# The two row blocks of the largest expert, cut into small units and spread between the other experts

## The chip, the core and the metric

The kernel runs on one core of one Trainium2 chip. The metric is the device time in microseconds of one execution, as the median of several runs; smaller is better. The core's engines are PE (TensorE, matrix products), DVE (VectorE), ACT (ScalarE), POOL (GpSimd) and SP, whose queue issues the loads of weights; 16 DMA engines move the data. The engines run their own instruction lists in order and wait for one another by semaphores.

## What is computed

The reference runs two transformer blocks on 256 tokens of width 1024, in float32. The change touches the last part only, a mixture of eight experts in which each token goes to two:

```
def moe_swiglu(x, router_w, router_b, w1, w3, w2):
    logits = (x @ router_w) + router_b
    top_vals, top_idx = lax.top_k(logits, TOP_K)          # TOP_K = 2, N_EXPERTS = 8
    top_w = jax.nn.softmax(top_vals, axis=-1)
    gate = jnp.sum(jax.nn.one_hot(top_idx, N_EXPERTS) * top_w[..., None], axis=-2)
    out = jnp.zeros_like(x)
    for e in range(N_EXPERTS):
        out = out + gate[..., e:e + 1] * swiglu(x, w1[e], w3[e], w2[e])
    return out                                            # swiglu: (silu(x w1) * (x w3)) w2
```

`w1` and `w3` of an expert are 1024 x 1408, `w2` is 1408 x 1024: 3 x 1024 x 1408 x 4 bytes = 17.3 MB an expert.

## The kernel before

**Weights.** The class `Weights` streams all weights in the order of a plan that a dry run writes down. `load` (L195) sends a load on SP's queue into the raw ring, as soon as `room_for` finds its slot free. The raw ring is made of arenas: `raw` (8192 columns of 128 partitions in f32), and in the experts' phase also `rawx` (6144), `cpack` (2048) and `rawt` (2048). `convert` splits a piece into a high and a low part: ACT writes `wh` (L232), DVE subtracts and writes `wl` (L233), into one ring of 6144 columns for each part. A piece of `w1` or `w3` here is one row of 128 x 1408, one of `w2` is 128 x 1024. A slot of the raw ring is free again when DVE has read it, one of the converted ring when PE has used it.

**Products.** Tokens are gathered into row blocks. A full block holds 128 tokens and takes three passes of PE for each piece (x high by w high, x high by w low, x low by w high). A half block holds up to 64 tokens, with high and low part side by side, and takes two passes. In the listings L421 to L423 (helper `mm3`) are the passes of full blocks, L1575 and L1576 (`mm_block`) those of half blocks. `turned` transposes the hidden values of a block between `w3` and `w2` (L1590 for half blocks, L1603 for full ones) and splits them again on ACT and DVE.

**Order.** Expert 0 is known before routing and goes first. The others stand in places 0 to 6 by load: place 0 is the largest and has two blocks, a full one (index 0) and a half one (index `NE`); places 1 and 2 have full blocks, places 3 to 6 half blocks. `moe` runs expert 0 and then the places 1, 4, 5, 0, 6, 2, 3 one after the other (list `groups`). `whole` is a generator: the first four rows of `w1` of the next expert run between `w3` and `w2` of the one before, and the work of `turned` is spread over them, one step behind each row (`todo`). For place 0 its loads are groups of 768 or 640 columns, and both blocks use each converted piece at once. Place 3, the last, runs through `expert`, with loads of four rows of 512 columns, and the final sum and norm stand around it.

`fetch` gets a block's rows: POOL makes a one-hot matrix `Pm` (L1489, from `kept` for full blocks and from `half` for half ones), PE multiplies it with the row numbers (`gp`, L1540), DVE copies the result (L1550, L1551), and POOL gathers the rows by an indirect DMA (L1556); after ten further steps PE transposes them (L1564). `route_places` is a chain of small operations on POOL and DVE that wait for each other; the sorting of the places and of the rows of the results (L1441 to L1482) is part of it.

Of the kernel before, what the change touches and what calls it, by code (L numbers as in the profile page):

```python
# [28 lines left out]
P = 128  # L29
# [5 lines left out]
NE = 8  # L35
# [251 lines left out]
class Build:  # L287
# [1243 lines left out]
    def fetch(self, j, out, half=False, back=False):  # L1531
# [28 lines left out]
        xh, xl = self.xslot(), None if half else self.xslot()  # L1560
# [48 lines left out]
    def whole(self, W, blks, w1, w3, w2, places, hT0=None):  # L1609

        nc = self.nc
        nb = len(blks)
        c0 = FFE % 512 if hT0 else 0
        kt = 2 if nb == 2 or hT0 else 1
        groups = [[(c, min(512, FFE - c)) for c in range(c0, FFE, 512)]] if nb == 1 else [
            [(0, 384), (384, 384)], [(768, 384), (1152, 256)]]
        passes = sum(2 if blk[3] else 3 for blk in blks)  # L1620

        def rows(w, ps, cols, k0, k1):
            a = cols[0][0]
            n = sum(m for _, m in cols)
            for kk in range(k0, k1, kt):
                for k, (_, wh, wl) in enumerate(W.want(w, kk * P, kt, a, n), kk):
                    for (x, *_), pb in zip(blks, ps):
                        for p, (c, m) in zip(pb, cols):
                            self.mm_block(p, [v if v is None else v[:, k] for v in x], wh[:, 0, c - a:c - a + m],
                                          wl[:, 0, c - a:c - a + m], k == 0, k == KD - 1)  # L1630
                    W.done()
                    self.tick(0)
                    self.step()
                    if todo:
                        todo.popleft()()

        banks = lambda name, cols: [[self.bank([m], name) for _, m in cols] for _ in blks]
        hT = [[] for _ in blks]
        todo = self.pending

        def evict(ps, h):
            for (_, _, _, half), pb, hb in zip(blks, ps, h):
                for p, r in zip(pb, hb):
                    nc.scalar.activation(r[0], p, AF.Copy if half else AF.Silu)

        def turns(ps, h, cols):

            for (_, _, _, half), pb, hb in zip(blks, ps, h):
                for p, r, (_, m) in zip(pb, hb, cols):
                    if half:  # L1650
                        r.append(self.b2([m], "su"))
                        nc.scalar.activation(r[1], p, AF.Copy)
                    else:
                        nc.vector.tensor_mul(r[0], p, r[0])
            new = deque(self.turned(blks[i][3], r, m, hT[i]) for i, hb in enumerate(h) for r, (_, m) in zip(hb, cols))
            run = []
            while new or run:
                yield
                run = [v for v in run if next(v, "end") != "end"]
                if new:  # L1660
                    run.append(new.popleft())
                    next(run[-1])

        for g, cols in enumerate(groups):
            ps = banks("g", cols)
            k0 = 0
            if g == 0 and not hT0:
                k0 = 4
                todo = yield
                rows(w1, ps, cols, 0, k0)  # L1670
                yield
                todo = self.pending
            rows(w1, ps, cols, k0, KD)
            h = [[[self.b2([m], "sg")] for _, m in cols] for _ in blks]
            if hT0:
                th = hT0()
                hT[0] = [tuple(v[:, k] for v in th) for k in range(c0 // P)]
            while todo:
                todo.popleft()()
# [447 lines left out]
```

## Time and profile before

| what | value |
|---|---|
| time, median of 3 runs | 1344.3 us (1343.62 to 1344.4) |
| time of the profiled execution | 1344.31 us |
| its span, first to last instruction | 1342.5 us |
| PE, DVE, ACT busy in the span | 96%, 71%, 57% |
| mean granted PE clock | 0.994 |
| weights of the experts | 8 x 17.3 MB, from about 890 us on |

The profiled execution is as long as the median run, so its span can stand for the runs, with 1.8 us around it. A busy PE is not PE at its peak: the ends of matrix products are modelled and overlap, so the price of one is read from the distance of two starts. The experts' phase is the last third of the span, from 889.9 us (the first product with expert weights) on.

### The profile page before, as it was taken

What the parts mean: (1) busy time and instruction counts of PE and PEld (TensorE: products, weight loads), DVE (VectorE), ACT (ScalarE), POOL (GpSimd) and SP (SyncE); (2) the same over time, 40 slices, a digit from 0 to 9 for tenths busy, and PEclk for the clock granted to TensorE, in tenths of its full rate; (3) what the DMA queues carried; (4) which work ended last, traced back from release to release, by engine and by line L of the source; (5) the groups of instructions that cost most, each with busy time, mean ns of one, the idle gap of its engine ahead of it and who ended that gap; (6) DMA issues with size and microseconds to landing.
All of it is one profiled execution on the core that took longest, in us unless ns stands there. A gap on an engine that the chain in (4) does not pass through costs nothing. (4 is left out here: it accounts for less than half of the span.)

```text
span 1342.5 us, 20715 instructions
## 1 busy us (share of the span) xinstructions
PE 1293.2 (96%) x7987; PEld 1137.2 (85%) x7987; DVE 956.5 (71%) x1252; ACT 763.0 (57%) x1057; POOL 171.6 (13%) x226
## 2 busy tenths in 40 slices
PE   9999999999999999999999999998999999989994
PEld 6977899997998998999989989987786789868772
DVE  6796565556784878465566866786998986659987
ACT  5674554443664655354434656445688885668882
POOL 3401200001000201000001002027502111001011
PEclk9999999999999999999999999999999999999997
DMA  7635867552562466575545623558999999769993
GB/s 275 204 126 173 307 218 238 189 188 79 182 227 94 158 202 220 174 239 173 187 140 156 219 98 107 192 186 338 331 397 364 373 390 348 259 225 388 391 373 95
DMA packets 128596, 309.59 MB, mean 231 GB/s; under 512 B 7345, under 2 KB 22737, under 8 KB 128490
## 3 DMA queue, kind: packets, MB, share of 16 engines
q1 hardware_dynamic: 121274, 287.65, 61.1%
q0 software_dynamic: 5424, 17.40, 4.4%
q10 hardware_dynamic: 1792, 3.15, 0.6%
q8 instruction: 64, 1.05, 0.3%
q14 instruction: 42, 0.34, 0.1%
HBM read 294.24 MB, written 10.78 MB: 227 GB/s over the span
## 5 line engine op out<-in xcount | busy, mean ns | idle before, releaser
L233 DVE TENSOR_TENSOR wl<-raw,wh 128x1024 fp32r<-128x1024 f32 (+4 forms) x338 | 395.1, 1194 | 157.4 <-ACT wh L232 151.9
L232 ACT ACTIVATE wh<-raw 128x1024 fp32r<-128x1024 f32 (+4 forms) x338 | 339.9, 1029 | 199.1 <-PE tr L495 99.8
L494 PE MATMUL tr<-xTh,wh 128*128 128x256 f32 x816 | 232.5, 285 | 0.0
L496 PE MATMUL tr<-xTh,wl 128*128 128x256 f32 x816 | 230.7, 283 | 0.0
L495 PE MATMUL tr<-xTl,wh 128*128 128x256 f32 x816 | 230.7, 283 | 0.0
L494 PEld LDWEIGHTS tr<-xTh,wh 128*128 128x128 f32 x816 | 156.3, 192 | 1.2
L495 PEld LDWEIGHTS tr<-xTl,wh 128*128 128x128 f32 x816 | 156.3, 192 | 0.5
L496 PEld LDWEIGHTS tr<-xTh,wl 128*128 128x128 f32 x816 | 156.3, 192 | 0.0
L233 DVE TENSOR_TENSOR wl<-rawx,wh 128x1024 fp32r<-128x1024 f32 (+4 forms) x85 | 106.9, 1291 | 16.7 <-ACT wh L232 16.7
L233 DVE TENSOR_TENSOR wx<-raw,wx 128x1024 fp32r<-128x1024 f32 (+1 forms) x56 | 65.6, 1185 | 49.2 <-ACT wx L232 49.2
L232 ACT ACTIVATE wh<-rawx 128x1024 fp32r<-128x1024 f32 (+4 forms) x85 | 91.7, 1110 | 15.1 <-PE u L1575 5.4
L232 ACT ACTIVATE wx<-raw 128x1024 fp32r<-128x1024 f32 (+1 forms) x56 | 56.4, 1030 | 49.2 <-PE tr L495 25.5
L495 PE MATMUL tr<-xTl,wx 128*128 128x256 f32 x240 | 67.5, 281 | 0.0
L494 PE MATMUL tr<-xTh,wx 128*128 128x256 f32 x240 | 67.4, 281 | 0.0
L496 PE MATMUL tr<-xTh,wx 128*128 128x256 f32 x240 | 67.4, 281 | 0.0
L529 POOL TENSOR_SCALAR rs<-lnmv 128x1 f32<-128x1 f32 x10 | 7.8, 782 | 455.4 <-DVE lnmv L576 455.4
L421 PE MATMUL nat<-wh,xTh 128*128 128x512 f32 (+1 forms) x152 | 60.5, 398 | 0.0
L422 PE MATMUL nat<-wl,xTh 128*128 128x512 f32 (+1 forms) x152 | 58.8, 387 | 0.7 <-DVE wl L233 0.4
L423 PE MATMUL nat<-wh,xTl 128*128 128x512 f32 (+1 forms) x152 | 58.7, 386 | 0.1
L1576 PE MATMUL u<-wl,xgh 128*128 128x384 f32 (+1 forms) x104 | 39.5, 384 | 6.3 <-DVE wl L233 6.2
L494 PEld LDWEIGHTS tr<-xTh,wx 128*128 128x128 f32 x240 | 45.2, 189 | 0.1
L495 PEld LDWEIGHTS tr<-xTl,wx 128*128 128x128 f32 x240 | 45.2, 188 | 0.1
(510 smaller groups left out, 3043.0 us busy)
## 6 DMA issues: line engine op xcount, KB each, us to landing
raw<-in_w_in SPq DMA_DIRECT2D x43, 1024.0 KB, 6.7
raw<-in_moe_w SPq DMA_DIRECT2D x44, 704.0 KB, 6.0
raw<-in_ffn_w SPq DMA_DIRECT2D x30, 1024.0 KB, 5.0
rawx<-in_moe_w SPq DMA_DIRECT2D x26, 1024.0 KB, 8.9
raw<-in_moe_w SPq DMA_DIRECT2D x17, 1024.0 KB, 10.1
rawx<-in_moe_w SPq DMA_DIRECT2D x23, 704.0 KB, 9.4
raw<-in_moe_w SPq DMA_DIRECT2D x14, 768.0 KB, 14.4
raw<-in_w_gate SPq DMA_DIRECT2D x10, 1024.0 KB, 5.2
```

The lines of the kernel that those rows point to most:

```text
L232: nc.scalar.activation(hi[:, :kn, :n], src, AF.Copy)
L233: nc.vector.tensor_sub(lo[:, :kn, :n], src, hi[:, :kn, :n])
L421: mm(out, xh, wh, start=start, stop=False)
L422: mm(out, xh, wl, start=False, stop=False)
L423: mm(out, xl, wh, start=False, stop=stop)
L494: mm(o, a, xh[:, kb + k], start=first and j % 2 == 0, stop=False, **kw)
L495: mm(o, a, xl[:, kb + k], start=False, stop=False, **kw)
L496: mm(o, b, xh[:, kb + k], start=False, stop=(kb + k == kt - 1), **kw)
L529: nc.gpsimd.tensor_scalar(out, ms, eps, None, op0=OP.add)
L1576: self.nc.tensor.matmul(out, x[0], wl, start=False, stop=stop)
```

## The change

`whole` is no longer a generator and has one block only. The largest expert (place 0) leaves the list; its two blocks run in a generator of its own, `beside_experts`, in units: two rows of `w1` or `w3` by 512 (or 384) columns, or two rows of `w2` by 512 columns, for both blocks. `fill` adds credit behind each row of another expert (0.17 for a full block, 0.34 for a half one), at the end of `w1` and `w3` (1) and behind each step of `turned` (0.7), and runs one step of the generator for each whole credit, as soon as both blocks are fetched. The order of the others is 4, 1, 5, 2, 6, 3. The first four rows of the next expert no longer run between `w3` and `w2`. The arena `rawx` is gone; the space goes to two more slots for gathered rows (`xs`) and to 22 instead of 14 tiles of 512 columns. Of the loads of expert weights there are 197 instead of 156, since `w2` comes in single rows and place 0 in units.

```
-    def whole(self, W, blks, w1, w3, w2, places, hT0=None):
...
-        kt = 2 if nb == 2 or hT0 else 1
-        groups = [[(c, min(512, FFE - c)) for c in range(c0, FFE, 512)]] if nb == 1 else [
-            [(0, 384), (384, 384)], [(768, 384), (1152, 256)]]
...
-            if g == 0 and not hT0:
-                k0 = 4
-                todo = yield
-                rows(w1, ps, cols, 0, k0)
-                yield
-                todo = self.pending
...
+    def whole(self, W, blk, w1, w3, w2, r0, fill, hT0=None):
+        x, _, gate, half = blk
         c0 = FFE % 512 if hT0 else 0
+        cols = [(c, min(512, FFE - c)) for c in range(c0, FFE, 512)]
+        rate = 0.34 if half else 0.17
+
+        def behind():
+            W.done()
+            self.tick(0)
+            self.step()
+            if self.pending:
+                self.pending.popleft()()
+            fill(rate)
+
+        def rows(w, ps):
+            for k in range(KD):
+                (_, wh, wl), = W.want(w, k * P, 1, c0, FFE - c0)
+                for p, (c, m) in zip(ps, cols):
+                    self.mm_block(p, [v if v is None else v[:, k] for v in x], wh[:, 0, c - c0:c - c0 + m],
+                                  wl[:, 0, c - c0:c - c0 + m], k == 0, k == KD - 1)
+                behind()
+
+        ps = [self.bank([m], "g") for _, m in cols]
+        rows(w1, ps)
+        fill(1)
...
+        ps = [self.bank([m], "u") for _, m in cols]
+        rows(w3, ps)
+        fill(1)
+        for _ in self.turns(blk, ps, h, [m for _, m in cols], hT):
+            fill(0.7)
+        acc = [self.bank([512], "eacc") for _ in range(2)]
+        for k in range(FFE // P):
+            (_, wh, wl), = W.want(w2, k * P, 1, 0, D)
...
+            behind()
...
+    def turns(self, blk, ps, h, ms, hT):
+        for p, r, m in zip(ps, h, ms):
+            self.evict2(blk[3], p, r, m)
+        for r, m in zip(h, ms):
+            yield
+            yield from self.turned(blk[3], r, m, hT)
...
+    def beside_experts(self, W, blks, w1, w3, w2, places):
+        cols = [(c, min(512, FFE - c)) for c in range(0, FFE, 512)]
         hT = [[] for _ in blks]
+        def up(w, name, c, m):
+            ps = [self.bank([m], name) for _ in blks]
+            for k in range(0, KD, 2):
+                (_, wh, wl), = W.want(w, k * P, 2, c, m)
+                for (x, *_), p in zip(blks, ps):
+                    for j in range(2):
+                        self.mm_block(p, [v if v is None else v[:, k + j] for v in x], wh[:, j], wl[:, j],
+                                      k + j == 0, k + j == KD - 1)
                 W.done()
                 self.tick(0)
+                yield
+            return ps
+        for c, m in cols:
+            ps = yield from up(w1, "g", c, m)
...
+            ps = yield from up(w3, "u", c, m)
+            for blk, p, r, t in zip(blks, ps, h, hT):
+                yield from self.turns(blk, [p], [r], [m], t)
+                yield
+        for hf in range(2):
+            acc = [self.bank([512], "eacc") for _ in blks]
+            for k in range(0, FFE // P, 2):
+                kn = min(2, FFE // P - k)
+                (_, wh, wl), = W.want(w2, k * P, kn, hf * 512, 512)
...
     def moe(self, x, xT, T):
-        self.phase("moe", 0, 14, 7)
-        self.W.arenas += [self.tmp.tile([P, 6144], F32, name="rawx", tag="rawx", bufs=1), self.cpack[:, :2048]]
+        self.phase("moe", 0, 22, 7)
+        self.W.arenas.append(self.cpack[:, :2048])
-        groups = [[1], [4], [5], [0, NE], [6], [2], [3]]
+        order = [4, 1, 5, 2, 6, 3]
...
+        tb = self.spawn(late([0, NE], mine, lambda: next(big)))
+        tg = self.spawn(late(order[:1], gots[0], self.xslot, 4))
+        side, credit = [], [0.0]
+
+        def fill(n):
+            if not side and mine and tb not in self.threads:
+                side.append(self.beside_experts(self.W, mine, *[(n, 0, "p0") for n in names], [YROW[0], P]))
+            credit[0] = min(credit[0] + n, 2.0)
+            while side and side[0] and credit[0] >= 1:
+                credit[0] -= 1
+                if next(side[0], "end") == "end":
+                    side[0] = None
```

The first place is on POOL, in the chain of routing behind expert 0's first products (`kept` makes the one-hot matrix of a full block, `half` that of a half one; `ybase` and `yv` belong to the rows of the results).

```order
 L1436 TENSOR_SCALAR pg<-pg 128x2
 L1489 TENSOR_SCALAR Pm<-kept,pg 128x128 x2
+L1489 TENSOR_SCALAR Pm<-half,pg 128x128 x2
 L1441 TENSOR_SCALAR ybase<-kept 128x8
 L1442 MEMSET ybase 128x1
```

The half block of place 0 is now fetched together with the full one, so a second pair of one-hot operations stands ahead of the rest of the chain. A few rows on, POOL also has a second gather and the pair of place 4:

```order
 L1475 COPY route<-route 128x8
+L1489 TENSOR_SCALAR Pm<-half,pg 128x128 x2
 L1478 TENSOR_SCALAR route<-kept,route 128x8
 L1479 TENSOR_TENSOR ptmp<-route 128x40
```

This pair stood behind the whole chain before and now stands within it.

The second place is on PE, in place 0's products with `w2` of the kernel before (10592 and 10593 are the halves of the full block, 10594 and 10595 those of the half one).

```order
L421 MATMUL eacc_10592<-wh_65,hTh_10325 128x512
L422 MATMUL eacc_10592<-wl_69,hTh_10325 128x512
L423 MATMUL eacc_10592<-wh_65,hTl_10326 128x512
L421 MATMUL eacc_10593<-wh_65,hTh_10325 128x512
L422 MATMUL eacc_10593<-wl_69,hTh_10325 128x512
L423 MATMUL eacc_10593<-wh_65,hTl_10326 128x512
L1575 MATMUL eacc_10594<-wh_65,hT_10389 128x512
L1576 MATMUL eacc_10594<-wl_69,hT_10389 128x512
L1575 MATMUL eacc_10595<-wh_65,hT_10389 128x512
L1576 MATMUL eacc_10595<-wl_69,hT_10389 128x512
```

These ten are one row of `w2`, and eleven such rows stand behind one another. In the changed kernel a unit of place 0 (8940 is its full block, 8941 the half one; seven of its ten products stand here) stands between rows of `w1` of place 4 (9069 to 9071):

```order
L421 MATMUL g_8940<-wh_65,xgl_8335 128x512
L422 MATMUL g_8940<-wl_69,xgl_8335 128x512
L423 MATMUL g_8940<-wh_65,xs_8336 128x512
L1575 MATMUL g_8941<-wh_65,xs_8337 128x512
L1576 MATMUL g_8941<-wl_69,xs_8337 128x512
L1575 MATMUL g_8941<-wh_65,xs_8337 128x512
L1576 MATMUL g_8941<-wl_69,xs_8337 128x512
L1575 MATMUL g_9069<-wh_65,xgl_8335 128x512
L1576 MATMUL g_9069<-wl_69,xgl_8335 128x512
L1575 MATMUL g_9070<-wh_65,xgl_8335 128x512
L1576 MATMUL g_9070<-wl_69,xgl_8335 128x512
L1575 MATMUL g_9071<-wh_65,xgl_8335 128x384
```

About every third row of a half block, and every sixth of a full one, such a unit follows. Its first units stand in expert 0's `w2`, its last in `w3` of place 2.

The third place is on PE too, at the turn from `w3` to `w2` of place 5 before (9908 is the transposed part of its hidden values; 9865 to 9868 are products of place 0's first rows).

```order
L1590 MATMUL tp_9908<-half_8328,sg_9787 128x64 x4
L1590 MATMUL tp_9908<-half_8328,su_9887 128x64 x4
L421 MATMUL g_9865<-wh_65,xgl_8333 128x384
L422 MATMUL g_9865<-wl_69,xgl_8333 128x384
L423 MATMUL g_9865<-wh_65,xgl_8333 128x384
L421 MATMUL g_9866<-wh_65,xgl_8333 128x384
L422 MATMUL g_9866<-wl_69,xgl_8333 128x384
L423 MATMUL g_9866<-wh_65,xgl_8333 128x384
```

At the turn of place 4 in the changed kernel (9346, 9372 and 9393 are its own transposes, 9331 and 9360 those of place 0's two blocks, 9400 the next unit's product):

```order
L1603 MATMUL tp_9331<-ident_88,sg_9148 128x128 x4
L1590 MATMUL tp_9346<-half_8330,sg_9216 128x64 x4
L1590 MATMUL tp_9346<-half_8330,su_9336 128x64 x4
L1590 MATMUL tp_9360<-half_8330,sg_9150 128x64 x4
L1590 MATMUL tp_9360<-half_8330,su_9355 128x64 x4
L1590 MATMUL tp_9372<-half_8330,sg_9218 128x64 x4
L1590 MATMUL tp_9372<-half_8330,su_9338 128x64 x4
L1590 MATMUL tp_9393<-half_8330,sg_9220 128x64 x3
L1590 MATMUL tp_9393<-half_8330,su_9340 128x64 x3
L421 MATMUL g_9400<-wh_65,xgl_8335 128x512
```

Place 0 turns at the same point, so the transposes stand behind one another there without a row of products between them.

## Rows read from the trace of the kernel before

**Rows 1.** Page, section 2: 40 slices of the span, DMA in tenths and in GB/s.

```profile
DMA  7635867552562466575545623558999999769993
GB/s 275 204 126 173 307 218 238 189 188 79 182 227 94 158 202 220 174 239 173 187 140 156 219 98 107 192 186 338 331 397 364 373 390 348 259 225 388 391 373 95
```

**Rows 2.** Windows of the experts' phase: stretch, busy time of each engine, clock, DMA.

```profile
core 0: us, PE busy (x) PEld busy (x) DVE busy (x) ACT busy (x) POOL busy (x), PEclk, DMA share, GB/s
...
900.00:960.00 60.00, 54.78 (x295) 47.26 (x294) 45.76 (x80) 37.59 (x46) 37.12 (x72) 1.00 0.88 322
960.00:1130.00 170.00, 164.42 (x833) 136.98 (x832) 145.24 (x143) 133.45 (x157) 31.65 (x18) 1.00 1.01 380
1130.00:1210.00 80.00, 73.73 (x403) 63.19 (x402) 50.50 (x54) 49.37 (x64) 6.14 (x5) 1.00 0.73 251
1210.00:1310.00 100.00, 97.23 (x481) 79.11 (x480) 89.86 (x88) 82.94 (x99) 12.13 (x9) 1.00 1.04 385
1310.00:1320.00 10.00, 8.50 (x38) 5.98 (x38) 8.98 (x11) 7.38 (x11) 1.55 (x1) 1.00 0.60 165
```

**Rows 3.** Timeline of PE, first products behind each expert's last `w2` row (start, duration).

```profile
945.24 0.48 PE L421 MATMUL g<-wh,xgl 128*128 128x512 f32 x1
...
955.06 0.40 PE L421 MATMUL eacc<-wh,hTh 128*128 128x512 f32 x1
...
971.52 0.50 PE L421 MATMUL g<-wh,xgl 128*128 128x512 f32 x1
...
1019.17 0.50 PE L1575 MATMUL g<-wh,xgh 128*128 128x512 f32 x1
...
1063.21 0.50 PE L1575 MATMUL g<-wh,xgh 128*128 128x512 f32 x1
...
1106.52 0.44 PE L421 MATMUL g<-wh,xgl 128*128 128x384 f32 x1
...
1191.25 0.47 PE L1575 MATMUL g<-wh,xgh 128*128 128x512 f32 x1
```

**Rows 4.** Timeline of PE: seven products in succession, and transposes of a half block.

```profile
950.87 0.39 PE L423 MATMUL g<-wh,xgl 128*128 128x512 f32 x1
...
951.78 0.33 PE L421 MATMUL g<-wh,xgl 128*128 128x384 f32 x1
...
952.30 0.50 PE L1540 MATMUL gp<-pg,Pm 128*128 128x2 f32 x4
...
1086.35 1.00 PE L1590 MATMUL tp<-half,sg 128*128 128x64 f32 x8
1087.18 1.06 PE L1590 MATMUL tp<-half,su 128*128 128x64 f32 x8
1088.05 0.42 PE L421 MATMUL g<-wh,xgl 128*128 128x384 f32 x1
```

**Rows 5.** Groups by line and form, 880 us on: DVE's share of a conversion.

```profile
L233 DVE TENSOR_TENSOR wl<-raw,wh 128x1408 fp32r<-128x1408 f32 x44 | 70.5, 1627 | 21.4 <-ACT wh L232 19.0 <-DMA cpack<-in_moe_w 1.5 <-DMA yd<-y 0.8
L233 DVE TENSOR_TENSOR wl<-rawx,wh 128x1024 fp32r<-128x1024 f32 x53 | 62.8, 1221 | 7.5 <-ACT wh L232 7.5
```

**Rows 6.** Waits of SP's queue from 880 us on: total us, times, longest.

```profile
SPq L195 <- DVE wl L233: 220.0, 110, 22.2
```

**Rows 7.** Timelines of PE, DVE and POOL in the chain of routing.

```profile
924.42 0.38 PE L1540 MATMUL gp<-pg,Pm 128*128 128x2 f32 x2 [1.32 <-POOL Pm L1489]
...
925.89 0.17 DVE L1451 MAX8 yhas<-yv 128x8 f32<-128x8 f32 x1 [1.91 <-POOL yv L1450]
...
921.32 3.05 POOL L1489 TENSOR_SCALAR Pm<-kept,pg 128x128 f32<-128x128 f32 x2
...
931.67 1.89 POOL L1556 DMA_INDIRECT xrows<-xd,islot  x1 [0.82 <-DVE gslot L1551]
...
945.87 2.57 POOL L1489 TENSOR_SCALAR Pm<-half,pg 128x128 f32<-128x128 f32 x2
...
956.72 9.46 POOL L1489 TENSOR_SCALAR Pm<-half,pg 128x128 f32<-128x128 f32 x2
```

More of the change, by code (lines that the diff above doesn't have):

```diff
@@ L1529, in gather, with fetch @@
         nc.scalar.activation(PT, tp.rearrange("p a b -> p (a b)"), AF.Copy)
-    def fetch(self, j, out, half=False, back=False):
+    def fetch(self, j, out, slot, half=False, back=False):
         nc = self.nc
@@ L1559, in fetch @@
             yield
-        xh, xl = self.xslot(), None if half else self.xslot()
+        xh, xl = slot(), None if half else slot()
         for k0 in range(0, KD, 4):
@@ L1718, in whole @@
-        self.pending.extend(lambda i=i, hf=hf: back(i, hf) for i in range(nb) for hf in range(2))
-        yield
+                yield
+            return ps
+        for c, m in cols:
+            ps = yield from up(w1, "g", c, m)
+            h = [[] for _ in blks]
+            for (_, _, _, half), p, r in zip(blks, ps, h):
+                self.evict(half, p, r, m)
+            ps = yield from up(w3, "u", c, m)
+            for blk, p, r, t in zip(blks, ps, h, hT):
+                yield from self.turns(blk, [p], [r], [m], t)
+                yield
@@ new lines, in beside_experts @@
+        for hf in range(2):
+            acc = [self.bank([512], "eacc") for _ in blks]
+            for k in range(0, FFE // P, 2):
+                kn = min(2, FFE // P - k)
+                (_, wh, wl), = W.want(w2, k * P, kn, hf * 512, 512)
+                for p, t in zip(acc, hT):
+                    for j in range(kn):
+                        self.mm_block(p, t[k + j], wh[:, j], wl[:, j], k + j == 0, k + j == FFE // P - 1)
+                W.done()
+                self.tick(0)
+                yield
+            for (_, _, g, half), p, r0 in zip(blks, acc, places):
+                self.back(half, g, p, r0, hf)
@@ L1940, in add, with late @@
             nc.vector.tensor_add(x2[t][:, sl], x2[t][:, sl], comb[t][hf])
-        def late(js, got):
+        def late(js, got, slot, delay=0):
             while not self.placed:
                 yield
-            gens = [self.fetch(j, got, half=3 <= j <= NE, back=j in groups[-1]) for j in js]
+            for _ in range(delay):
+                yield
+            gens = [self.fetch(j, got, slot, half=3 <= j <= NE, back=j == order[-1]) for j in js]
             while gens:
@@ L1966, in moe @@
                 break
-            tg = self.spawn(late(groups[i + 1], fetched[i + 1]))
-            new = self.whole(self.W, got, *ws, [YROW[js[0]], P])
-            next(new)
-            new.send(todo)
-            for _ in run:
-                pass
-            run = new
+            tg = self.spawn(late(order[i + 1:i + 2], gots[i + 1], self.xslot))
+            self.whole(self.W, gots[i][0], *ws, YROW[j], fill)
+        got = gots[-1]
+        last = self.expert(self.W, got, *ws)
+        next(last)
         g, b = (self.vec(a[f"ln2_{v}_2"][1]) for v in "gb")
```

138 lines of the change are left out of this document (42 added, 96 removed).

## Prediction

> **What bounds the kernel now.** I read the page's slices first: in the experts' phase DMA stands at nine tenths and 330 to 400 GB/s, as nowhere earlier, with one hollow, 259 and 225 GB/s, in the slices behind 1140 us [rows 1]. The windows sharpen this [rows 2]: DMA's share is 1.01 and 1.04 in the stretches 960 to 1130 and 1210 to 1310 us, at 380 and 385 GB/s, but 0.73 at 251 GB/s between 1130 and 1210, where PE has the larger part of 80 us. I call 385 GB/s the full rate. The timeline of PE says which expert stands there [rows 3]. From the end of one expert's `w2` to the end of the next: place 1 takes 47.7 us (971.52 to 1019.17), place 4 44.0, place 5 43.3, and place 0 84.7 (1106.52 to 1191.25). An expert's 17.3 MB take 45 us at the full rate, so the half blocks run at the pace of the transfers, and place 0 doesn't: it has 75 us of products for the same bytes (below).
>
> While PE is slow, the raw ring fills, and SP can send nothing until DVE has freed a slot: it waited 220.0 us for that in the phase [rows 6]. A bound by PE thus shows as a hollow in DMA that is never made up, since the next experts need the full rate. Its size: 80 us x (385 - 251) = 10.7 MB, or 28 us. That is the most that spreading place 0 can give back. A second, smaller hollow lies between 900 and 960 us (322 GB/s, 10 us missing), during routing.
>
> **Prices.** Four products of 512 columns start in 0.91 us and three of 384 in 0.52 [rows 4]: 0.228 and 0.173 each. A row of `w1` or `w3` is 2 x 0.228 + 0.173 = 0.63 a pass, a row of `w2` 0.456. With 16 and 11 rows, a pass costs 15.1 us: 45.2 for a full block, 30.1 for a half one, 75.3 for place 0. Around the products each turn costs transposes: sixteen of a half block's 44 take 1.70 us [rows 4], so 4.7 in all. From the intervals, corrected for the four rows of the next expert in them: place 1 took 47.7 + 7.5 (its own four, full) - 5.0 (place 4's four) = 50.2, which is 5.0 over its products; place 0 took 84.7 + 7.0 - 5.0 = 86.7, or 11.4 over. A half block's overhead is hidden behind transfers; I take 5.5, the transposes and 0.8 for its fetch. DVE needs 16 x 1.63 + 11 x 1.22 = 39.5 us an expert [rows 5], so it follows the transfers closely, but doesn't lead.
>
> **The change part by part.**
>
> *The start loses about 9 us.* Expert 0 ended at 971.52, with four rows of place 1 inside, 945.24 to 955.06 [rows 3]; without them, and with the 0.8 us of transposes that stood among them, it ends at 962.5. Two pairs of one-hot operations and a second gather now stand in POOL's chain. DVE waits in order for that chain (1.91 us at 925.89), its conversions queue behind the waiting operation, and PE waits for the first pair (1.32 us at 924.42) and then for conversions [rows 7]. A pair took 2.57 us once and 9.46 another time; I take 2.57, since DVE itself waits there, and 1.3 for the gather (the first took 1.89): 6.5 us. The turn of expert 0 has no cover any more, since the units don't exist yet and place 4's rows come later: two products' worth of DVE work, 2 us by half of the 1.22 of a conversion each and a split. Expert 0 ends at 971, apart from units that run in it early.
>
> *The middle is bound by PE.* Place 4 with its share of units needs 30.1 + 5.5 + 17.5 of 57 steps of place 0's 86.7, or 62 us, against 17.3 + 5.3 MB, 59 us at the full rate; place 1 with 10.8 steps needs 66 us against 53. So the ring stays full and PE's sum decides, for places 4, 1, 5, 2 and 0: 2 x 50.2 + 2 x 35.6 + 86.7 = 258 us. Place 0's larger overhead is kept: its transposes and splits remain, and three of its turns stand on top of those of places 4, 1 and 5. The end of place 2's `w2` comes at 971 + 258 = 1229. The smaller loads (197 for 156) and SP's extra issues cost nothing here, because SP waits for slots anyway; without that cover they would add to the 59 us.
>
> *The end is bound by DMA.* Place 0's last unit stands in `w3` of place 2, so at 1229 - 11 x 6 x 0.228 = 1214 only place 2's `w2` and places 6 and 3 are left, 40.4 MB, and a half block needs 36 us of PE for 45 of transfer. The full ring holds less than before: 12288 raw columns are 7 pieces of 1408, 5.0 MB (12 pieces of 1024, 6.3 MB, in `w2`), and the converted ring adds 2.9 to 3.1; I take 8.7 MB, where before 11 raw pieces made 10.8. To load: 31.7 MB, and about 6 MB of results, gathers and vectors (before, from 1191.25 to 1320 DMA moved 45 MB by the windows, 7 more than the 38.2 MB of weights that a full ring would have left): 37.7 MB at 385 GB/s is 98 us, to 1312. Before, DMA's last stretch moved 1.65 MB behind 1310, so it ended at 1314 [rows 2]. What follows, the last rows, the sum and the norm, is untouched.
>
> **The sum.** Of the 28 us that the hollow holds, the start takes 9 and the smaller ring 7 to 8; the overlapping turns and the end without units take most of the rest. The span changes by 1312 - 1314 = -2 us, to 1340.5, and with the 1.8 us around it the time is **1342 us**. The profiled execution is as long as the median run. A change of 0.2%, 2.7 us, is about what a measurement of this kernel tells from none.
>
> **The rivals.**
>
> *A, the sum above*, chance 0.42, with 1333 to 1350 for its own range: each of its three terms is uncertain by 3 to 5 us. Faster 0.20, same 0.16, slower 0.06.
>
> *B, the hollow closes without new waits*, 0.25. If spare time of DVE behind POOL absorbs the 6.5 us at the start, and units stand where experts wait, PE's sum falls towards its products and transposes: 225.8 + 2 x 1.2 + 3 x 4.7 + 1.2 + 6 for fetches = 249.5, 8.5 less than 258. That gives 1342 - 6.5 - 8.5 = 1327. For it: place 0's products alone are only 75.3 of 86.7, and DVE idled in the hollow (50.50 of 80 us [rows 2]). Against it: the turns stay. The Trainium skill (Perfetto Trace Analysis, Optimization Strategy) says that where the most contended engine changes between regimes, interleaving them may help; by that rule the whole hollow would close, 28 us less the ring's 7.5, and the time would be some 1324. This trace shows the two regimes, 0.73 and 1.04 of DMA, and so what the rule asks for.
>
> *C, POOL's pairs are long*, slower, 0.15. If each pair takes the 9.46 us seen at 956.72, where DVE converted without a break, instead of 2.57, the chain, and with it the conversions and PE, come 13.8 us later: 1356. It decides from about 5 us a pair on. For it: both durations stand in the trace [rows 7]. Against it: at this place DVE is idle, waiting for POOL. The Trainium skill (Perfetto Trace Analysis, Optimizing Scalar/DVE Operations) says that GpSimd and DVE share an SBUF read port; the two durations agree with that, but no row shows the port itself.
>
> *D, the turns stand in each other's way*, mostly slower, 0.12. At three turns place 0's transposes and splits stand directly beside the other expert's, without products between, so that PE waits through ACT's and DVE's chain, where before four rows (5 to 7 us) stood between. At 4 us more each the time is 1354; it decides from 2 us each on.
>
> *E, no change because transfers bind throughout*, 0.06: if units cost PE less than I think, the ring never fills and only the start and the end remain, 1344.
>
> **How the numbers follow.** Faster: 0.20 + 0.25 + 0.02 = 0.47. Same: 0.16 + 0.04 + 0.01 = 0.21. Slower: 0.06 + 0.15 + 0.11 = 0.32. B's and C's centres must lie inside the range, with some room, for it to hold 8 in 10: 1323 to 1357.
>
> **What would show it.** Right: expert 0's `w2` ends (without units) near 971; DMA's share lies between 0.85 and 0.95 from 975 to 1210, without a hollow of 0.73, and at 1.0 behind; PE's products of place 2's `w2` end near 1229; DMA ends near 1312. The pair of one-hot operations from `half` behind the first pair should take 2 to 4 us, and PE wait 3 to 4 us at `gp`. Wrong: DMA at full share from 975 on (E, or B if place 2 ends before 1218); expert 0 ending behind 980 (C); gaps of more than 4 us on PE at the first L1590 or at the first `w2` product behind the turns of places 4, 1 and 5 (D); or last products of place 0 behind place 2's `w3`, which would move the bound of the end to PE.

## The result: 1356 us, 0.97% slower

| | before | changed |
|---|---|---|
| time, median of 4 runs | 1344.0 us | 1356.3 us (1355.4 to 1360.1) |
| ratio, 95% interval | | 1.0097 (1.0077 to 1.0116) |
| profiled execution, its span | 1344.3, 1342.5 us | 1355.4, 1353.7 us |
| mean granted PE clock | 0.994 | 0.987 |

The page's slices of DMA, in tenths and GB/s, and the wait of SP's queue for freed slots from 880 us on (total, times, longest), for [rows 1, 6]:

```profile
DMA  7635976552661566575535723656799989999992
GB/s 273 202 125 171 320 226 217 180 187 80 217 218 63 187 207 214 160 238 190 186 99 175 230 94 125 211 203 221 234 397 346 362 311 394 336 365 338 398 357 92
```
```profile
SPq L195 <- DVE wl L233: 247.9, 142, 17.6
```

The two slices of 259 and 225 GB/s are gone, but the two from 914 to 981 us (221 and 234) are far below those of the kernel before (338 and 331), and SP waits more for slots than it did (247.9 for 220.0 us). The windows of the changed kernel, for the stretches of [rows 2] (the busy times of PE, its weight loads, DVE, ACT and POOL, then the clock, DMA's share and GB/s):

```profile
core 0: us, PE busy (x) PEld busy (x) DVE busy (x) ACT busy (x) POOL busy (x), PEclk, DMA share, GB/s
900.00:960.00 60.00, 49.24 (x254) 42.38 (x253) 38.03 (x77) 30.11 (x40) 32.57 (x76) 0.91 0.74 250
960.00:1130.00 170.00, 169.40 (x834) 142.70 (x832) 141.24 (x129) 129.36 (x144) 18.16 (x11) 1.00 0.93 338
1130.00:1210.00 80.00, 78.92 (x399) 67.05 (x398) 66.59 (x65) 59.40 (x68) 4.76 (x4) 1.00 0.97 358
1210.00:1310.00 100.00, 93.98 (x423) 70.10 (x422) 81.83 (x78) 78.17 (x94) 14.85 (x11) 0.97 1.01 368
1310.00:1320.00 10.00, 6.88 (x35) 4.94 (x33) 6.78 (x8) 6.07 (x8) 1.57 (x1) 1.00 1.05 346
1320.00:1330.00 10.00, 6.48 (x22) 4.01 (x23) 6.49 (x8) 6.41 (x8) 0.00 (x0) 1.00 0.51 194
```

The hollow of 251 GB/s is filled (358), as meant. But the routing stretch fell from 322 to 250 GB/s, and the stretch 960 to 1130, where the kernel before had 380, has 338. PE is busy there for 169.40 of 170 us: one deep hollow has become a shallow one that lasts from 960 to 1210. DMA ends near 1325, not 1314: the last window's 10 x 194 = 1.9 MB take 5.6 us at the 346 GB/s of the window ahead of it.

Three windows make the ledger that the experiments are read by. First the kernel before, then the changed one:

```profile
890.00:985.00 95.00, 88.43 (x457) 75.49 (x458) 74.78 (x115) 60.01 (x71) 47.62 (x81) 1.00 0.84 312
985.00:1210.00 225.00, 213.16 (x1119) 179.75 (x1118) 175.64 (x181) 163.52 (x201) 31.61 (x21) 1.00 0.91 334
1210.00:1320.00 110.00, 105.73 (x517) 85.08 (x516) 98.84 (x98) 90.32 (x109) 13.69 (x10) 1.00 1.00 365
```
```profile
890.00:985.00 95.00, 82.89 (x414) 70.03 (x413) 65.44 (x112) 48.88 (x62) 36.89 (x84) 0.95 0.68 228
985.00:1210.00 225.00, 223.31 (x1119) 189.92 (x1118) 189.39 (x176) 172.88 (x195) 22.92 (x15) 1.00 0.97 358
1210.00:1320.00 110.00, 100.86 (x456) 75.04 (x454) 88.61 (x85) 84.24 (x102) 16.41 (x12) 0.97 1.01 366
```

Up to 985 us the changed kernel moved 95 x 84 = 8.0 MB less, 20.7 us at the full rate of 385 GB/s. Up to 1210 it won back 225 x 24 = 5.4 MB.

Where the start goes: PE's and POOL's timelines (start, duration, and in brackets the wait and its releaser).

```profile
939.14 1.16 PE L1540 MATMUL gp<-pg,Pm 128*128 128x2 f32 x4 [6.27 <-POOL Pm L1489]
940.17 2.91 PE L1942 MATMUL hg<-Pm,sg 128*128 128x128 f32 x12
942.73 0.77 PE L421 MATMUL u<-wh,xgh 128*128 128x512 f32 x1
```
```profile
932.56 2.02 POOL L1556 DMA_INDIRECT xrows<-xd,islot  x1 [0.82 <-DVE gslot L1551]
934.87 0.94 POOL L1556 DMA_INDIRECT xrows<-xd,islot  x1 [0.30 <-issue]
...
936.64 1.12 POOL L1470 CAST order<-noverf 128x1 int32<-128x1 f32 x1 [0.26 <-DVE noverf L1468]
...
938.48 1.19 POOL L1489 TENSOR_SCALAR Pm<-half,pg 128x128 f32<-128x128 f32 x2
```
```profile
930.00:940.00 10.00, 3.73 (x16) 2.81 (x14) 3.75 (x11) 2.87 (x4) 8.21 (x21) 0.84 0.78 257
940.00:950.00 10.00, 10.00 (x43) 8.71 (x44) 7.32 (x14) 5.49 (x6) 5.61 (x9) 0.79 0.74 251
```

PE stands 6.27 us at the third fetch, that of place 4. Its one-hot pair is short (1.19 us), but on POOL it stands behind both gathers and the sorting of places. Expert 0's `w3` begins at 942.73; in the kernel before it began at 931.47.

PE's timeline from there on. 961.02 and 963.35 are the starts of two units in expert 0's `w2`, 2.33 us apart (a third begins at 975.24). The other rows are the first product of place 4, of place 0's units behind place 2's `w3`, of place 2's `w2` and of place 6, each the end of what stood ahead:

```profile
961.02 0.39 PE L421 MATMUL g<-wh,xgl 128*128 128x512 f32 x1
963.35 0.39 PE L421 MATMUL g<-wh,xgl 128*128 128x512 f32 x1
...
981.76 0.39 PE L1575 MATMUL g<-wh,xgl 128*128 128x512 f32 x1
...
1205.15 0.39 PE L421 MATMUL eacc<-wh,hTh 128*128 128x512 f32 x1
...
1216.75 0.48 PE L421 MATMUL eacc<-wh,hTh 128*128 128x512 f32 x1
1233.16 0.39 PE L1575 MATMUL g<-wh,xgl 128*128 128x512 f32 x1
```

What DMA still moved from 1216.75 to 1330, in all and on the queue of weights:

```profile
DMA packets 14947, 39.38 MB, mean 348 GB/s; under 512 B 978, under 2 KB 3026, under 8 KB 14937
...
q1 hardware_dynamic: 13081, 34.28, 81.4%
```

The last units don't stand in place 2's `w3`, as was said of the change, but in its turn: `w3` ends at 1205.15, and from there to 1216.5 nearly five units and place 2's transposes take turns on PE. ACT waits in order for those transposes, and the conversions behind them wait too. From 1216.75 on SP's queue waits for slots (total, times, longest, up to 1233), and DMA falls while place 2's `w2` runs:

```profile
1210.44 0.60 ACT L505 ACTIVATE hTh<-tp 128x512 fp32r<-128x512 f32 x1 [2.40 <-PE tp L1603]
...
1215.54 0.60 ACT L505 ACTIVATE hTh<-tp 128x512 fp32r<-128x512 f32 x1 [3.54 <-PE tp L1603]
```
```profile
SPq L195 <- DVE wl L233: 15.6, 7, 5.5
```
```profile
1216.75:1233.16 16.41, 15.72 (x69) 12.40 (x68) 14.23 (x13) 14.20 (x16) 4.78 (x3) 1.00 0.89 288
```

### The profile page after: what moved, and what is told of

It reads as the page before. It is cut to its first block, busy times and chain, and to the rows that moved or that the text cites. A ratio compares the mean times of both kernels' runs of the same rounds, so it can differ in the third digit from the quotient of the medians.

```text
span 1353.7 us, 20705 instructions
## 1 busy us (share of the span) xinstructions
PE 1299.1 (96%) x7907; PEld 1135.7 (84%) x7907; DVE 957.6 (71%) x1241; ACT 761.6 (56%) x1044; POOL 154.4 (11%) x226
## 3 DMA queue, kind: packets, MB, share of 16 engines
q1 hardware_dynamic: 125562, 287.65, 61.3%
## 5 line engine op out<-in xcount | busy, mean ns | idle before, releaser
L233 DVE TENSOR_TENSOR wl<-raw,wh 128x1024 fp32r<-128x1024 f32 (+3 forms) x396 | 473.5, 1220 | 165.0 <-ACT wh L232 163.3
L232 ACT ACTIVATE wh<-raw 128x1024 fp32r<-128x1024 f32 (+3 forms) x396 | 406.3, 1049 | 217.7 <-PE tr L495 98.0
L233 DVE TENSOR_TENSOR wl<-cpack,wh 128x1024 fp32r<-128x1024 f32 (+3 forms) x34 | 45.1, 1346 | 9.7 <-ACT wh L232 9.4
L233 DVE TENSOR_TENSOR wl<-rawt,wh 128x1024 fp32r<-128x1024 f32 (+2 forms) x34 | 43.8, 1311 | 3.8 <-ACT wh L232 3.7
L232 ACT ACTIVATE wh<-cpack 128x1024 fp32r<-128x1024 f32 (+3 forms) x34 | 38.4, 1153 | 14.1 <-PE g L423 7.5
```

What stands on the lines that cost most here:

```text
L232: nc.scalar.activation(hi[:, :kn, :n], src, AF.Copy)
L233: nc.vector.tensor_sub(lo[:, :kn, :n], src, hi[:, :kn, :n])
```

## The experiments

All ratios are to the kernel before. Differences under 2 us between variants are not read.

### The ring and the start, one by one

**e1**, place 4's block first, those of place 0 sixteen steps later:

```
-        tb = self.spawn(late([0, NE], mine, lambda: next(big)))
-        tg = self.spawn(late(order[:1], gots[0], self.xslot, 4))
+        tg = self.spawn(late(order[:1], gots[0], self.xslot))
+        tb = self.spawn(late([0, NE], mine, lambda: next(big), 16))
```

> The row block of place 4 is fetched first, and the two blocks of place 0 sixteen steps later; nothing else differs from the change. Theory 1 (the start: the fetch of three blocks at once puts PE behind POOL's queue, where it stood 6.27 us at 939.14 in the changed kernel's trace): that wait goes, the rows of w3 of expert 0 begin near 933 instead of 942.73, and the time falls by 8 to 11 us, to 1345 to 1348. Theory 2 (the smaller ring of raw weights and the end are what costs): the rows of w3 begin earlier, but the time stays within 3 us of 1356. Theory 3 (the middle is full on PE and on DMA at once, and takes what the start gives): between the two, 1349 to 1353.

Measured: 1353.8 us, 1.0065 (1.0051 to 1.0078), 2.5 us off the change. The wait is gone and `w3` begins at 931.69. A new wait takes part of its place, at the turn, and expert 0 ends at 968.64, without units:

```profile
931.69 0.48 PE L421 MATMUL u<-wh,xgh 128*128 128x512 f32 x1
...
949.83 1.47 PE L1603 MATMUL tp<-ident,sg 128*128 128x128 f32 x6 [4.07 <-DVE sg L1619]
...
968.64 0.39 PE L1575 MATMUL g<-wh,xgl 128*128 128x512 f32 x1
```

DMA moved 263 instead of 228 GB/s up to 985, 3.3 MB or 8.6 us more, and then 350 instead of 358 and 352 instead of 366 in the ledger's later windows: what the start gains is lost behind it. Theory 1 alone doesn't hold.

**e2**, the kernel before without `rawx`; **e3**, the change with 3072 columns of ring given back:

```
-        self.W.arenas += [self.tmp.tile([P, 6144], F32, name="rawx", tag="rawx", bufs=1), self.cpack[:, :2048]]
+        self.W.arenas += [self.cpack[:, :2048]]
```
```
-        self.phase("moe", 0, 22, 7)
-        self.W.arenas.append(self.cpack[:, :2048])
+        self.phase("moe", 0, 16, 7)
+        self.W.arenas += [self.tmp.tile([P, 3072], F32, name="rawx", tag="rawx", bufs=1), self.cpack[:, :2048]]
```

> The kernel before without its 6144 extra columns for raw weights, as the change removes them; nothing else differs. Theory 2 (the ring's smaller size costs 7 to 8 us, the prediction's own figure: 3.1 MB at 385 GB/s): 1351 to 1352. Theory 1 (only the start counts): 1344 to 1346, since the hollow behind 1130 us refills a ring of any size and the end alone feels it.

> The change with 3072 columns of raw ring given back, taken from the small buffers (16 instead of 22). Theory 2: two more pieces of 1408 columns lie ahead when DMA becomes the bound, 1.4 MB or 3.7 us: 1352 to 1353. Theory 1: 1355 to 1357, no change, as the start is untouched. A longer time would say that the 22 small buffers were needed.

Measured: e2 1351.8 us, 1.0055 (1.0041 to 1.0069), 7.7 us slower than before; e3 1351.6 us, 1.0053 (1.0040 to 1.0067), 4.7 us off the change. The ring's price is that of the prediction. In e2 the first window fell from 312 to 282 GB/s, 2.8 MB, about the 3.1 MB that were taken away:

```profile
890.00:985.00 95.00, 89.76 (x457) 76.49 (x457) 74.74 (x116) 59.77 (x70) 45.59 (x81) 0.98 0.77 282
```

So of the 20.7 us that the change lacks by 985, the ring is 7.4, if it costs there what it costs in e2, and the start, by difference, 13.3.

**e5**, e1 and e3 together; **e11**, 4608 columns of ring, with 13 small buffers; **e12**, that ring and place 0's fetch six steps later:

> Both edits together: the two blocks of place 0 fetched sixteen steps later, and 3072 columns of raw ring given back. Alone they gave 2.5 and 4.7 us. If the start and the ring are separate losses, the gains add: 1348 to 1350. Theory 4 (the products' own sum is the bound once the ring is large enough: 344 us from the end of expert 0's w2 to the end of place 3's, by the prediction's prices; the kernel before took 354.9 so, with 962.5 for that end without the rows of place 1, after 352.2 with 974.7, the larger ring alone 347.5 with 976.1): the earlier end of expert 0, 968.6, is carried through with an excess of 4 us, place 3 ends near 1317 instead of 1323.6, and the time is 1344 to 1346. If the start's gain is lost again, as it mostly was alone: 1351 to 1352.

> The change with 4608 columns of raw ring given back (13 small buffers instead of 22), three pieces of 1408 where 3072 hold two. If each piece is worth its transfer, as two gave 4.7 us: 1349 to 1350. If the small buffers or the start now bind: 1351 to 1353.

> The same ring, and place 4's block fetched first, those of place 0 six steps behind it, so that the wait of 6 us at the start goes and units still run beside expert 0's w2 (sixteen steps took them away from there, and the units then ended 18 us later). If the start's gain was lost through the late units: 1344 to 1347. If a head start of PE is worth nothing once the transfers bind the end: 1349 to 1351, as with the ring alone.

Measured: e5 1351.4 us, 1.0049 (1.0035 to 1.0062), no better than the ring alone; e11 1359.2, 1.0112 (1.0096 to 1.0129), and e12 1359.3, 1.0111 (1.0094 to 1.0128). Both missed all that was expected (1344 to 1353): they are no faster than the change (their medians are 3 us above it, within its spread of 1355.4 to 1360.1), and the later fetch gave nothing. The 344 us of theory 4 counted place 3 as a full block; with a half one the products' sum is 329.5, which leaves an excess of 18 to 25 us in the three kernels, so this theory was no bound at all. In e11 PE waited for a conversion in place 2, 3.28 us at 1200.32. Whether fewer small buffers hold ACT up there was not tried apart.

### The pace of the units

**e4**, rates of 0.13 and 0.26; **e6**, 0.22 and 0.44; **e7**, no units in the turns and 0.27 and 0.49 beside rows:

```
-        rate = 0.34 if half else 0.17
+        rate = 0.26 if half else 0.13
```
```
         for _ in self.turns(blk, ps, h, [m for _, m in cols], hT):
-            fill(0.7)
+            pass
```

> The change with its units at rates of 0.13 and 0.26 instead of 0.17 and 0.34, so that some ten of 57 steps move from places 4, 1 and 5 into places 2 and 6. Theory 3 (the middle is bound by PE while the end is bound by DMA with PE idle): places 4, 1 and 5 end about 12 us earlier, DMA carries more there, and the time falls by 5 to 10 us, to 1346 to 1351. Theory 1: within 3 us of 1356, since the delay of the start is only carried along. If place 6 becomes bound by PE: slower than 1357.

> The change with its units at rates of 0.22 and 0.44 instead of 0.17 and 0.34, so that they end in place 5 or early in place 2. Slower units cost 8.3 us. Theory 4 (the sum of the products binds while units last, the transfers behind): an earlier end of the units lengthens the stretch that the transfers bind, and the time grows by 0 to 5 us, to 1356 to 1361. If late units are what costs (place 2 and 6 overfull, and the transfers idle beside them): 1350 to 1354.

> The change with no units during the turns of the other experts, and rates of 0.27 and 0.49 beside the rows, which give as many units an expert. Rival D of the prediction (the turns stand in each other's way): three turns of places 4, 1 and 5 get shorter, and the time falls by 3 to 8 us. If the units in the turns are cover for PE's waits on the chain of ACT and DVE: waits of 2 to 4 us on PE at the transposes of each turn, and 1360 to 1366.

Measured: e4 1364.6 us, 1.0156 (1.0142 to 1.0170); e6 1359.8, 1.0117 (1.0102 to 1.0133); e7 1358.8, 1.0104 (1.0089 to 1.0119). e4 and e6 are slower than the change, by 8.3 and 3.5 us; e7 is 2.6 us above it, but its runs (1356.4 to 1359.2) lie within the change's, so that it is only not faster. Theory 3 in its simple form fails. Two windows of e4:

```profile
1210.00:1250.00 40.00, 39.88 (x177) 31.71 (x177) 31.97 (x28) 29.85 (x31) 7.44 (x4) 1.00 0.90 309
1250.00:1290.00 40.00, 36.89 (x161) 30.37 (x159) 29.15 (x29) 29.22 (x39) 0.90 (x1) 0.83 0.94 347
```

Its late units stand in place 2, a full block for which PE itself needs longer than the transfers, and in place 6 up to 1256: PE is busy for 39.88 of 40 us and DMA falls to 309 GB/s, from 348 in the change. Then PE stood for 2.50 us at a turn (1268.70) and its clock fell to 0.83. In e7 the time doesn't fall without units in the turns, but this is no clean test of rival D: its units end in place 6, at 1248.96, 32 us later than the change's, and e4 shows that late units cost. Nor were the units cover for long waits in the turns, as the other theory had it: PE's longest at a transpose of the middle is 1.04 us (1153.14). In e6 the units end by 1193, ahead of place 2's turn, and DMA keeps 377 GB/s from 1210 to 1250; it is slower all the same, with 348 GB/s instead of 358 from 985 to 1210.

### The transfers' rows

**e8**, the kernel before with loads cut at 512 columns:

```
-            self.b.nc.sync.dma_start(raw[:, k:k + step], w[:, k:k + step])
+            cut = 512 if isinstance(name[-1], str) else n
+            for c in range(0, n, cut):
+                self.b.nc.sync.dma_start(raw[:, k:k + step, c:min(c + cut, n)], w[:, k:k + step, c:min(c + cut, n)])
```

> The kernel before with every load of its placed experts' weights cut into columns of 512, so that the transfers' rows are 2 KB as those of the change's units, with two to three times as many loads; nothing else differs. If rows of 2 KB slow the transfers (the changed kernel's 355 GB/s at a share of 0.96 would be 92% of 385): DMA moves 350 to 360 GB/s between 985 and 1130, where it moved 379, and the time grows by 15 us or more. If the size of the rows makes no difference: 379 and 1343 to 1346.

The change's units load rows of 512 columns, 2 KB, where place 0's loads of `w1` and `w3` had 768 or 640; e8 asks what shorter rows cost. Measured: 1362.2 us, 1.0127 (1.0112 to 1.0143), 18 us slower. From 985 to 1130, first e8, then the kernel before, both with DMA at a share of 1.00:

```profile
DMA packets 29135, 49.71 MB, mean 343 GB/s; under 512 B 2543, under 2 KB 9259, under 8 KB 29122
```
```profile
DMA packets 14804, 54.96 MB, mean 379 GB/s; under 512 B 1280, under 2 KB 1280, under 8 KB 14794
```

If bytes and packets have a price each, 14331 packets more and 5.25 MB less fill the same 145 us: 0.88 ns of the core's DMA time a packet. The whole change adds few of them (125,562 for 121,274 on the queue of weights): 3.8 us by this estimate. e8 has more loads too, and row length and number of loads were not tried apart.

### PE's work taken away

**e9**, the change, and **e10**, the kernel before, with one product for each block of place 0 instead of three and two, so that place 0's outputs are less exact (e10's edit is the same, where a group has two blocks):

```
-                        self.mm_block(p, [v if v is None else v[:, k + j] for v in x], wh[:, j], wl[:, j],
-                                      k + j == 0, k + j == KD - 1)
+                        self.nc.tensor.matmul(p, x[0][:, k + j], wh[:, j], start=k + j == 0, stop=k + j == KD - 1)
...
-                        self.mm_block(p, t[k + j], wh[:, j], wl[:, j], k + j == 0, k + j == FFE // P - 1)
+                        self.nc.tensor.matmul(p, t[k + j][0], wh[:, j], start=k + j == 0, stop=k + j == FFE // P - 1)
```

> The change with the units' products of the low halves left out (one product instead of three for the full block of place 0, one instead of two for its half block), so that the outputs of place 0 are less exact; loads, conversions and order stay. By the prices this takes 45 us from PE between 960 and 1216. If PE binds that stretch: DMA reaches 375 to 385 GB/s there instead of 355, place 2's w2 ends 10 to 15 us earlier, and the time falls by 8 to 14 us, to 1342 to 1348. If the units' transfers in rows of 2 KB or waits of SP bind it: DMA stays at 350 to 365 and the time falls by less than 4 us.

> The kernel before with the products of the low halves left out for the two blocks of place 0 alone (45 us of PE's work, the outputs of place 0 less exact); all else stays. It takes the work away that made the hollow of DMA between 1130 and 1210. If the hollow is worth the 28 us of the prediction: 1316 to 1320. If the experts ahead of it and behind it have so little room that PE's sum or DVE decides there, the gain stays under 20 us: 1325 to 1335.

Measured: e9 1340.4 us, 0.9968 (0.9956 to 0.9981), more than was expected; e10 1321.0, 0.9819 (0.9802 to 0.9835), between its two cases. The same work on PE is worth 23.4 us in the kernel before and 15.9 in the change. This is the reading that settles most: **the change hides 7 to 8 us of PE's work, and pays 19.4 us that stay when most of this work is gone.** e10, then e9:

```profile
890.00:985.00 95.00, 90.04 (x458) 76.72 (x458) 75.12 (x115) 60.53 (x71) 45.33 (x81) 0.98 0.86 316
985.00:1210.00 225.00, 203.60 (x1003) 167.10 (x1002) 197.25 (x205) 183.86 (x228) 35.54 (x22) 0.95 0.97 370
```
```profile
890.00:985.00 95.00, 82.66 (x412) 70.02 (x413) 67.32 (x114) 51.51 (x66) 36.02 (x84) 0.93 0.69 235
985.00:1210.00 225.00, 207.46 (x967) 164.96 (x966) 192.63 (x182) 177.69 (x203) 24.91 (x15) 0.97 0.97 367
```

Behind 985 they are alike (370 and 367). Before it lie 81 x 95 us = 7.7 MB or 20 us: the whole 19.4.

**e13** and **e14**, e9 with the later fetch of e1, and with the ring of e3 as well:

> Units of one product as before (the outputs of place 0 less exact), and the two blocks of place 0 fetched sixteen steps later. With this little work on PE the transfers bind from 985 us on, and there the change stood 19.4 us behind the kernel before with the same cut. If the start is that loss beside the ring (95 us at 235 instead of 316 GB/s up to 985, 7.7 MB or 20 us, of which the ring is 8): the later fetch gives 6 to 9 us here where it gave 2.5 with all products, 1331 to 1335. If the start's gain is lost in any case: 1338 to 1341.

> The same with 3072 columns of raw ring given back. If start and ring together are the 19.4 us: 1327 to 1330, 4 to 5 us below the one with the later fetch alone, and what is left to 1321 is the other half of the ring. If transfers in rows of 2 KB cost more than the 4 us that the packets' count allows: it stays at 1332 or above.

Measured: e13 1330.8 us, 0.9893 (0.9879 to 0.9907); e14 1328.2, 0.9883 (0.9869 to 0.9898). Here, where transfers bind, the later fetch gives 9.5 us, with 264 instead of 235 GB/s in the first window (2.8 MB, 7.2 us), against 2.5 us in e1. So the start's loss is real:

```profile
890.00:985.00 95.00, 83.17 (x430) 70.15 (x429) 72.22 (x120) 57.84 (x70) 46.98 (x87) 0.98 0.75 264
```

e14 came where it was put, but by a smaller step (2.7 us for 4 to 5). 7 us to e10 remain, of which half the ring is some 4; the turn's wait that e1 showed may be the rest.

### The order of the places

**e15**, place 6 ahead of place 2; **e16**, that with the edits of e1 and e3; **e17**, e16 with eleven steps instead of sixteen; **e18**, e17 with 0.30 instead of 0.34:

```
-        order = [4, 1, 5, 2, 6, 3]
+        order = [4, 1, 5, 6, 2, 3]
```

> The change with place 6 ahead of place 2 (4, 1, 5, 6, 2, 3 instead of 4, 1, 5, 2, 6, 3), so that the last units stand beside place 6, a half block that has 9 us of room on PE, and a full block comes behind it. Theory 5 (the change leaves the room of places 6 and 3 unused, and the transfers then bind an end of 34.6 MB): the units end 20 us later in place, one half block less stands in the bound end, and the time falls by 6 to 14 us, to 1342 to 1350. If late units cost by themselves, as the slower rates did: 1357 to 1365.

> That order, with the later fetch and the 3072 columns of ring. Theory 5: a head start of PE now counts, since PE binds up to place 2: another 5 to 9 us off the order alone, 1335 to 1342, faster than the kernel before. If the end is bound by transfers as ever: 1349 to 1352, as without the new order.

> As the last (order 4, 1, 5, 6, 2, 3, ring, later fetch), with eleven steps instead of sixteen, so that the products of the two fetches stand ahead of the turn of expert 0, where PE waited 4.06 us, and the units come some 5 rows earlier. If that wait and the empty w2 of expert 0 are the rest of the start's loss: 1339 to 1343, faster than the kernel before. If PE then waits for the pairs of POOL instead (they took 4.99 and 2.96 us and ended at 949.3): 1344 to 1347.

> The same with the units beside half blocks at a rate of 0.30 instead of 0.34, so that the last few stand in place 2. If the room of the half blocks is what the units should fill, and PE has none beside place 2 (38.7 of 40 us busy between 1210 and 1250): 2 to 5 us slower than the run with 0.34. If the transfers alone bind behind 1210: the same or 1 to 2 us faster.

Measured: e15 1351.1 us, 1.0052 (1.0040 to 1.0064); e16 1344.4, 0.9998 (0.9989 to 1.0007); e17 1344.5, 0.9999 (0.9990 to 1.0008); e18 1351.9, 1.0052 (1.0039 to 1.0066). The order gives 5.2 us alone (with 377 GB/s from 1210 to 1250, 348 in the change), and 7.0 on top of the other two edits, which had stopped at 1351.4. e16 stays 2 us above what was expected of it. Its first window:

```profile
890.00:985.00 95.00, 84.93 (x434) 72.02 (x433) 71.40 (x118) 55.91 (x68) 46.98 (x87) 0.96 0.77 273
```

Up to 985 it still lacks 39 x 95 us = 3.7 MB or 9.6 us to the kernel before, and is level with it all the same: by this ledger the spreading is worth about as much in this order. e17 shows one wait taking another's place (`gp` at 948.63, 5.54 us for POOL's pair, instead of the turn's 4 us). e18 is 7.4 us slower than e17, but not for the reason it was made for: none of its units came to stand in place 2. They end in place 6's turn near 1216.6, over 7 us later than in e17 (1209.0), so what it shows is that units that last longer cost time there too. The order has a second reading that no run parts from the room beside place 6: it also takes the units out of place 2's turn, where they held up the conversions. No version with all the products beat the kernel before.

## Why the prediction was wrong

Forecast were 1342 us, measured 1356: 14 us more, and slower instead of the same.

**The start: mis-sized, and by another wait.** It was to lose 9 us, from 962.5 to 971 for expert 0's end without units. That end came at 981.76 with three units of 2.33, or 974.8: 12.3 us. The second pair of one-hot operations, which carried the sum and rival C, took 1.17 us instead of 2.57 and cost PE little (1.30 us at the first `gp`, as in [rows 7], and 0.19 at the next two), though the granted clock then fell to 0.51 from 927 to 930. What was missed stands in order in PE's list: place 4's `gp`, behind POOL's gathers and sorting. No rival had it, and C's 1356 is right by accident. Nor do its two durations speak for a shared port, as C's text has it: beside the pair of 2.57 us DVE was converting as well (946.35 to 947.97).

**The middle: right.** 258 us were forecast for places 4, 1, 5, 2 and 0. From 981.76 to 1233.16 are 251.4 us; with the three units that ran earlier, 258.4. DMA's share of 0.93 and 0.97 there fits the 0.85 to 0.95 forecast but for a little, and place 2's `w2` ends at 1233, 4 us after the forecast: the start's miss, carried along.

**The end: the step that failed.** "37.7 MB at 385 GB/s is 98 us, to 1312" carries nearly all of the miss: DMA ended near 1325, 13 us later. It began 3 us late (1216.75 instead of 1214), there were 39.38 MB left, 1.7 MB or 4 us more, and these moved at 364 GB/s, not 385: another 6 us. The bytes: the ring was reckoned as full with 8.7 MB; of the 40.4 MB of weights still to be used then, 34.28 were not yet moved, so 6.1 had landed (results and gathers were 0.9 MB less than reckoned). The ledger points the same way: of the 8.0 MB behind at 985, 5.4 were won back by 1210 and 2.6 were not. The sum had taken the start as a delay of PE, and had let the end begin with a full ring all the same. SP was waiting for slots, which says that these were taken, in part by loads that had not landed. The rate: of the 6 us, 4 lie in place 2's `w2`, with 288 GB/s, behind the turn that held the units. The prediction had named last products behind place 2's `w3` as a sign of being wrong, and they came; but it was DVE and ACT, not PE, that they held up. That this turn is the cause of the 288 GB/s is read from the order of the waits and was not tried alone.

**The ring's own term, 7 to 8 us: right** (7.7 in e2).

**The hollow.** "28 us is the most that spreading place 0 can give back" was near the truth of what it is worth, 23.4 us (e10), and far from what this change fetched, 7 to 8. The prices of the prediction say part of why, and the sum should have said so plainly. A half block needs 35.6 us of PE for 45 of transfers, so it has room for 9.4; a full one has none (50.2). Place 0 has 41.7 too many (86.7 - 45). Spread over places 4, 1, 5 and 2, it finds 18.8 us of room, and the rest stays a hollow, only thinner: 258 us of PE for 5 x 45 = 225 of transfers. The room of places 6 and 3 lies behind the last unit, where the transfers bind. With place 6 moved ahead (e15, e16) the time falls, as it would if part of that room were used. Of the 18.8 us only 7 to 8 were found; where the other 11 went is open.

**Why the start's gain shows in e13 and hardly in e1 and e5.** In e13 the transfers bind from 985 on, and bytes moved earlier are time saved. In e1 PE is full from 985 to 1210 (222.78 of 225 us busy), and its later units stand beside place 2 and at the front of place 6; the transfers fell behind there (352 GB/s from 1210 to 1320), as in e4. With place 6 ahead of place 2 the three edits together give 11.9 us. But this doesn't show that the order brings the start's gain back: e16 is 6.6 us faster than e15 by ring and later fetch, and the ring alone gave 4.7 in the other order, which leaves 2 us for the fetch, too little to be read. How much of e1's loss is the units' place and how much PE's own waits stays open.

**The rivals.** B (the hollow closes) failed with its mechanism: the Trainium skill (Perfetto Trace Analysis, Optimization Strategy) holds that interleaving regimes may help, and here it hid 7 to 8 us of 23.4, for 19.4 of cost. D, as priced, didn't come: PE showed no wait above 0.9 us at a turn in the middle of the changed kernel. What a turn with units held up, in place 2, was the conversions. E is refuted by e9: with less work on PE the middle went from 358 to 367 GB/s and the time fell.

## What to carry to other kernels

Before spreading work that one engine binds, add up the room in each stage that is to take it, stage by stage: by the prices here, stages that are over their own transfer time take nothing, and room that lies behind the last spread piece is lost. Take the sum as a ceiling: here 7 to 8 us came of 18.8. Count what the spreading needs first, buffers and earlier fetches, as transfer time at the place where the transfers bind. And look for the last wait in each engine's own order, not only for the longest operation: a short one behind a long queue stops the engine as well.

## What the runs showed of the hardware

Rows of 2 KB moved 343 GB/s where rows of mostly 4 to 5.6 KB moved 379, with DMA's share at 1.00 in both (e8, with more loads). The Trainium skill (Perfetto Trace Analysis, DMA Optimizations) says that larger transfers use the memory's bandwidth better, with 2 KB to 4 or 8 KB as its example; this trace agrees, with 10% between the two.

A stop of PE cost more than its length. Behind the 6.27 us at 939.14 the granted clock was 0.79 from 940 to 950, part of that stretch at the lower of the two levels (1.2 of 2.4 GHz), with PE busy throughout. It had fallen before, to 0.51 from 927 to 930, behind the waits of 1.30, 0.19 and 0.19 us at `gp`: products of 512 columns started 0.43 us apart there instead of 0.23. In the kernel before, one wait of 1.32 us at the same place [rows 7] left it at 1.00. In e4 it was 0.83 over 40 us with a wait of 2.50 us in them.

The pair of one-hot operations on POOL, the same instruction on the same shape, took 1.19 us at 938.48 in the changed kernel and up to 9.46 in the one before [rows 7]. DVE was waiting for POOL beside the first and converting beside the second, but it was converting too beside one of 2.57. No run here tells what the length hangs on.
